# Attention's PSUM in two kinds of places, and b gates and sigmoids in the order of the rows, in a hybrid encoder layer

## The chip, the cores and the metric

The kernel runs on one core of a Trainium2 chip. The metric is the device time of one execution in microseconds (us): the median of three runs before is 1467.02 us (1465.7 to 1467.43). A profile is one further execution, taken by the hardware profiler. Five engines work side by side, each through its own list of instructions in a fixed order: PE (matmuls; its weight loads are listed as PEld), DVE and ACT (elementwise work, and the only readers of matmul results), POOL and SP (here mostly starting DMAs). An instruction that waits holds up everything behind it on its engine. Matmuls write to PSUM, eight banks of 128 partitions x 512 floats, of which all eight are given out in the part of the program that changes.

## The reference, cut to what matters

1024 new frames of one stream and 64 frames of a running one go through one layer. A combined projection feeds a gated convolution and a band attention; both results are weighted with sigmoid gates and merged:

```python
proj = xn @ w_in                       # cb, cc, ch, q, k, v, ga, gb
ya = (cb * causal_conv(cc * ch)) @ w_conv_out
o = band_attend(q, k, v, ...)          # 8 heads of 64, bias by relative distance, softmax
yb = o.reshape(B, L, ATT_DIM) @ w_attn_out
merged = sigmoid(ga) * ya + sigmoid(gb) * yb
x = x + merged @ w_out                 # then RMSNorm, SwiGLU FFN, residual, RMSNorm
```

A frame sees its own chunk of 64 frames and the eight before it, so a tile of 128 frames needs at most 640 keys, five blocks of 128.

## The kernel before

All products are in float32, each made of three matmuls on operands split into a high and a low part (`split`, lines 128 and 129: ACT casts the high part, DVE subtracts it to get the low part). The channels of the gates that the convolution half needs early are done before; what is left for the middle of the kernel is the b gate of all eight row blocks of 128 channels and the a gate of row blocks 6 and 7.

**The gates and attention run together.** `gate(i, cs)` computes row block i of `GATES` in pieces of 272 frames: 24 matmuls (`product`, lines 343 to 345) into one of three PSUM banks of pool `pmm`. A b gate is copied by ACT (line 908) and stored to `gb_d` by POOL (line 909); of the last two row blocks (a gates 6 and 7, tiles named g8 and g9) ACT takes the sigmoid straight out of the bank into `ga_rows` (line 905). Between the pieces the program advances `attention()` by 3.15 steps (`PER`). One step issues `scores` of a query tile, `transposed` of the tile two steps back, and every other time `values` of a pair of tiles. A scheduler then fixes the order of each engine, from these dependencies and its own estimates.

**A tile of attention.** `scores` puts up to 640 scores into a place of two banks; DVE adds the bias and takes the row's extreme in one custom instruction (line 964), ACT takes the exponential (line 974). `transposed` turns up to five blocks of 128x128 weights on PE (line 1053) into a place of two banks, and `split` takes them out in one cast and one subtraction (`pt`). Both kinds share one pool: `patt` has two places of two banks, handed out in turn to s and t. `values` (line 1078) has the eighth bank, in `ppv`. After a head's ninth tile, `rt` turns the nine columns of reciprocal row sums, ACT copies them to `rows`, and POOL stores them in four DMAs to `rc_d` (lines 1040 and 1044).

**The end of attention.** At i = 8 the pools of attention are closed. `ob`, the attention's output as a matmul operand, takes their place: its quarters 0 and 1 are cast from `o_rows` (tile names o0 and o1), which were scaled earlier; quarters 2 and 3 are loaded from `o_d` (line 1170), multiplied on DVE with `rc2` and `rc3`, the sums loaded back from `rc_d` (lines 1090 and 1172), and cast by ACT. `rows_in(m)` loads row block m of the b gate into a tile gb (line 1138) and of y into yg (line 1139), four of them here. The merge loop then goes over `MERGE = [6, 7, 0, 1, 2, 3, 4, 5]`: a sigmoid of gb on ACT (line 1194), the yb product on PE, multiply and add on DVE. `tc.issue_after(x)` puts what is issued under it behind instruction x in the schedule.

Of the kernel before, what the change touches and what calls it, by code (L numbers as in the profile page):

```python
# [8 lines left out]
F32 = mybir.dt.float32  # L9
F32R = mybir.dt.float32r  # L10
AF = mybir.ActivationFunctionType
# [4 lines left out]
P = 128  # L16
# [3 lines left out]
TS = 64  # L20
# [46 lines left out]
def encoder_kernel(ctx: ExitStack, tc: tile.TileContext, ins, outs):  # L67
    nc = tc.nc
    mm = nc.tensor.matmul
    vec, act, pool_e = nc.vector, nc.scalar, nc.gpsimd  # L70
# [13 lines left out]
    ident = const.tile([P, P], F32, name="ident")  # L84
# [41 lines left out]
    def split(hi, lo, src):  # L126

        a = act.copy(hi, src)  # L128
        b = vec.tensor_tensor(lo, src, hi.bitcast(F32), op=ALU.subtract)  # L129
        return a.ins, b.ins  # L130
# [214 lines left out]
            newest[0] = mm(out, b, p, start=False, stop=k == kt - 1).ins  # L345

    PIECES = [(j * HN, HN) for j in range(4)]
    GATES = [("b", m) for m in range(8)] + [("a", m) for m in range(6, 8)]
    for g, m in GATES:
        if m % 2 == 0:  # L350
            base = (C_GA if g == "a" else C_GB) + m * P
            ld = {"src": w_in[:, base : base + 2 * P], "w": 2 * P}
        plan.append((ld, KD, m % 2 * P))
    MERGE = [6, 7, 0, 1, 2, 3, 4, 5]
    for m in MERGE[::2]:
        ld = {"src": ins["w_attn_out"][0][:, m * P : (m + 2) * P], "w": 2 * P, "at": 40}
        plan += [(ld, 4, j * P) for j in range(2)]
# [483 lines left out]
    for n in range(len(units)):  # L841
# [26 lines left out]
        for _ in r:  # L868
            if n == 12:
                uforms(si)  # L870
            if n < 2 and si in (2 + n, 5 + n):
                i = 2 * n + si // 5
# [20 lines left out]
    patt = att_stack.enter_context(tc.tile_pool(name="patt", bufs=2, space=PSUM, reuse_waits="tile"))  # L893
# [4 lines left out]
    def gate(i, cs):  # L898
        g, m = GATES[i]
        for c in cs:  # L900
            o, n = PIECES[c]
            ps = pmm.tile([P, 512], F32, tag="mm", name=f"g{i}_{c}")
            product(ps[:, :n], gate_w[i], xn, o, n)
            if i >= len(GATES) - LAST:
                act.activation(ga_rows[m - 6][:, o : o + n], ps[:, :n], AF.Sigmoid)  # L905
                continue
            st = st_pool.tile([P, HN], F32, tag="st", name=f"gst{i}_{c}")
            act.copy(st[:, :n], ps[:, :n])
            nc.gpsimd.dma_start(gb_d[m * P : (m + 1) * P, o : o + n], st[:, :n])

    gate_w = {}

    heads, sums = {}, {}

# [75 lines left out]

    def scores(h, t):
        q, k, ks, v, vs, bias = heads[h]
        ps = patt.tile([P, 2, 512], F32, tag="att", name=f"s{h}_{t}")
        s = at_pool.tile([P, 640], F32, tag="s", name=f"p{h}_{t}", bufs=4)
        if t < 8:
            nb = min(t + 1, 5)
            k0, n, r = (t - nb + 1) * P, nb * P, P
            q0 = t * P if t < 4 else t * P + TS
        else:
            k, k0, n, r = ks, 0, CACHE + TS, TS  # L1000
            q0 = 512
        parts = 2 if n > 512 else 1
        w = n // parts
        for i in range(parts):
            ksl = slice(k0 + i * w, k0 + (i + 1) * w)
            mm(ps[:r, i, :w], q[0][:, q0 : q0 + r], k[:, ksl], start=True, stop=False)
            mm(ps[:r, i, :w], q[1][:, q0 : q0 + r], k[:, ksl], start=False, stop=True)  # L1007
        b0 = 640 - n if t < 8 else 0
        if t == 0:
            sums[h] = sm2[:, h % 2]  # L1010
        sm = sums[h]
        softmax(
            s[:r, :n], ps[:r, :, :w] if parts == 2 else ps[:r, 0, :w], bias[:r, b0 : b0 + n], sm[:r, t : t + 1],
            f"{h}_{t}",
        )
        return s
# [1 line left out]
    pts = {}  # L1018

    def transposed(h, t, s):  # L1020
        tp = patt.tile([P, 2, 512], F32, tag="att", name=f"t{h}_{t}").rearrange("p a b -> p (a b)")
        if t == 8:
            pt = at_pool.tile([P, 2, 5, TS], F32R, tag="pts", name=f"pts{h}", bufs=1)
            for i in range(4):
                nc.tensor.transpose(
                    tp[:, i * TS : (i + 1) * TS], s[:TS, i * P : (i + 1) * P], ident[:TS, :TS]
                )
            nc.tensor.transpose(tp[:TS, 512 : 512 + TS], s[:TS, 512:576], ident[:TS, :TS])
            split(pt[:, 0, :4, :], pt[:, 1, :4, :], tp[:, : 4 * TS].rearrange("p (b t) -> p b t", t=TS))
            split(pt[:TS, 0, 4, :], pt[:TS, 1, 4, :], tp[:TS, 512 : 512 + TS])  # L1030
            pts[h, 4] = pt

            sm = sums.pop(h)
            vec.reciprocal(sm, sm)
            tr = patt.tile([P, 2, 512], F32, tag="att", name=f"rt{h}")[:9, 0, :P]
            nc.tensor.transpose(tr, sm, ident)
            rows = at_pool.tile([P, P], F32, tag="rows", name=f"rows{h}", bufs=1)[:9]
            act.copy(rows, tr)
            for e in range(2):
                nc.gpsimd.dma_start(  # L1040
                    rc_d[h, e * HT : e * HT + 512].rearrange("(t p) -> t p", p=P), rows[4 * e : 4 * e + 4]
                )
                c = e * HT + 512
                nc.gpsimd.dma_start(rc_d[h : h + 1, c : c + 32], rows[8:9, 32 * e : 32 * e + 32])
            return
        g, j = divmod(t, 2)
        if j == 0:
            pts[h, g] = at_pool.tile([P, 2, 6, 256], F32R, tag="pt", name=f"pt{h}_{g}")
        pt = pts[h, g]
        nb = min(t + 1, 5)  # L1050
        b0 = t - nb + 1 - max(0, 2 * g - 4)
        for i in range(nb):
            nc.tensor.transpose(tp[:, i * P : (i + 1) * P], s[:, i * P : (i + 1) * P], ident)
        src = tp[:, : nb * P].rearrange("p (b t) -> p b t", t=P)
        js = slice(j * P, (j + 1) * P)
        split(pt[:, 0, b0 : b0 + nb, js], pt[:, 1, b0 : b0 + nb, js], src)

    def values(h, t):
        q, k, ks, v, vs, bias = heads[h]
# [76 lines left out]
    def rows_in(m):  # L1136
        t, z = rows[m] = u_rows.tile([P, T], F32, tag="yg", name=f"yg{m}"), row_tile((MERGE.index(m) % 5 + 1) % 2, f"gb{m}")
        nc.sync.dma_start(z, gb_d[m * P : (m + 1) * P])
# [8 lines left out]
    for i in range(4):  # L1147
# [3 lines left out]
        if i == 0:  # L1151
            prep(5)
    for i in range(4, len(GATES)):
        gate_w[i] = next_w()
        if i == len(GATES) - LAST:
            for _ in steps:
# [4 lines left out]
            t = uo.tile([P, 2, 4 * T + 8], F32R, name="ob")[:, :, : 4 * T]  # L1161
            ob = Acts(t.rearrange("p l (k t) -> p l k t", k=4))
            u_rows = pg_stack.enter_context(tc.tile_pool(name="u_rows", bufs=5, reuse_waits="tile"))
            ga_rows = [uo.tile([P, T], F32, name=f"ga{m}") for m in (6, 7)]
# [3 lines left out]
            for k, r in zip((2, 3), late_r):  # L1168
                o = ob.t[:, 0, k].bitcast(F32)
# [6 lines left out]
        for c in range(4):  # L1176
            gate(i, (c,))
            between()
        if i >= len(GATES) - LAST:
            m = GATES[i][1]  # L1180
            t = rows[m][0]
# [7 lines left out]
    for n, m in enumerate(MERGE):  # L1189
        wb = next_w()  # L1190
        if n + 4 < 8:
            rows_in(MERGE[n + 4])
        t, z = rows.pop(m)
        act.activation(z, z, AF.Sigmoid)
        late = t.rearrange("p (h n) -> p h n", h=2)[:, :, 512:]
        hi, lo = (ms[:, m, l].rearrange("p (h n) -> p h n", h=2) for l in range(2))
        for h in range(2):
            yb = psum2.tile([P, 2, 512], F32, tag="mm", name=f"yb{m}_{h}")
            for j in range(2):
                if n == 0:  # L1200
                    with tc.issue_after(gates_end):
                        product(yb[:, j, :HN], wb, ob, h * HT + j * HN, HN)
                else:
                    product(yb[:, j, :HN], wb, ob, h * HT + j * HN, HN)
            hs = slice(h * HT, (h + 1) * HT)
            zh, th = z[:, hs], t[:, hs]
            two = zh.rearrange("p (j n) -> p j n", j=2)
            vec.tensor_tensor(two, yb[:, :, :HN], two, op=ALU.mult)
            vec.tensor_tensor(th, th, zh, op=ALU.add)
            split(mg.at(0, m, h * HT, HT), mg.at(1, m, h * HT, HT), th)  # L1210
        pool_e.tensor_copy(hi, late)
        pool_e.tensor_tensor(lo, late, hi.bitcast(F32), op=ALU.subtract)
# [65 lines left out]
    if True:  # L1278
# [5 lines left out]
        for i in (0, 1, 2, 3, 8, 4, 5, 6, 7):  # L1284
            t0, n = TT[i]
            xt = wp.tile([P, D], F32, tag="xg", name=f"xr{i}")[:, :512]
            nc.sync.dma_start(xt[:n], x_rows(i)[:, :512])
            ps = bank2("BD", f"wo0_{i}")[:, 0]
# [373 lines left out]
    for n in range(1, len(names)):  # L1662
# [7 lines left out]
        if 2 <= n < 18:  # L1670
            nm, src = (("k", ck), ("v", cvv))[(n - 2) // 8]
            a = (n - 2) % 8 * 56
# [21 lines left out]
    bufs = {(hp, "hs"): 1, (hp, "snap"): 3, (hp, "sa"): 4, (hp0, "snap"): 1, (hp0, "sa"): 1}  # L1694
    for n, (i, d) in enumerate(order):
        if n < len(homes):
            pool, tag = homes[n]
# [33 lines left out]
    for b, ks in enumerate(blocks):  # L1731
        first, final = b == 0, b == len(blocks) - 1
        nk = blocks[b + 1] if not final else []
        for g in range(2):
            ps = {}
# [27 lines left out]
            for si, js in turns:  # L1763
                p, ht = STEPS[si], hts[base + si]
                key = {1: "A", 6: "A", 5: "A", 3: "A", 2: "B", 7: "D", 4: "D"}[p]
                for j in js:
                    i = 2 * g + j
                    if (key, j) not in ps:
                        ps[key, j] = psD.tile(
                            [P, 512], F32, tag="A" if key == "A" else "BD", name=f"{key}{b}_{i}",  # L1770
                            bufs=2 if key == "A" else 4,
                        )
                    t = ps[key, j]
                    ends = final and g == 1 and js == (1,) and si == len(STEPS) - 1
                    for c in ((slice(0, 256), slice(256, 512)) if ends else (slice(0, 512),)):
# [8 lines left out]
                    h, d, fresh = {  # L1784
                        1: (0, 0, 1), 2: (0, 0, 0), 6: (1, 0, 1), 7: (1, 1, 1), 5: (1, 1, 0), 4: (1, 0, 0), 3: (0, 1, 1),
                    }[p]
                    o = acc[i + 4 * h, d]
# [7 lines left out]
                    if final and si == 2:  # L1795
                        for hh, dd in ((0, 0), (1, 1), (1, 0), (0, 1)):
                            a = acc[i + 4 * hh, dd]
# [71 lines left out]
```

## Time and profile before

| | |
|---|---|
| median of three runs | 1467.02 us (1465.7 to 1467.43) |
| the profiled execution | 1467.9 us, of which the span from the first to the last instruction is 1466.1 |
| mean granted PE clock | 0.997 |
| gates alone | 384.9 to 411.5 us of the span |
| gates with attention | 411.5 to 591.3 |
| the last gates | 591.3 to 616.3 |
| the yb products of the merge | 616.3 to 664.3 |

How to read it: a busy share of PE near 100% does not say that PE could not be faster, since the ends of matmuls are modelled and overlap; the start-to-start times of matmuls say how fast it goes. A row of a group has line, engine, operation, output<-input, shape, count, then busy time and mean ns of one, then the idle time just before them and what ended it. A row of a timeline has start in us, duration in us, the instruction, how often it follows itself, and in brackets the idle time before it and its releaser. Rows of engine SPq or POOLq are the issue of a DMA, not its landing.

### The profile page before, as it was taken

How to read it: one execution, taken by the hardware profiler on the slowest of the kernel's cores; microseconds unless marked ns; L12 is line 12 of the kernel's file. 1: busy time of each engine (PE TensorE's matmuls, PEld its weight loads, DVE VectorE, ACT ScalarE, POOL GpSimd, SP SyncE). 2: the span in 40 equal slices, each digit the busy share in tenths (PEclk: the TensorE clock that was granted, in tenths of full speed). 3: DMA queues.
4: the chain of work that ended last, by engine and by line, in shares of the span. 5: the costliest groups of instructions: out<-in, count | busy, mean ns of one | idle time of the engine just before them, and what ended most of it. 6: DMA issues, size and time to landing. Idle time of an engine off the chain costs nothing.

```text
span 1466.1 us, 26257 instructions
## 1 busy us (share of the span) xinstructions
PE 1449.1 (99%) x10137; PEld 1362.2 (93%) x10137; DVE 993.3 (68%) x1831; ACT 679.7 (46%) x1354; POOL 154.4 (11%) x282
## 2 busy tenths in 40 slices
PE   8999999999999999999999999999999999999997
PEld 6899999999999989998889999999999998888886
DVE  7975565658357767473588667766666668957676
ACT  7644343336367667431355444444344445512223
POOL 1400010001221121111100111111011111000000
PEclk9999999999999999999999999999999999999999
DMA  8687612235877675743432444443334449877685
GB/s 286 182 276 226 197 56 71 67 111 200 261 214 195 177 189 150 260 149 126 156 108 80 160 162 157 151 168 129 122 130 169 148 179 313 274 232 249 210 266 204
DMA packets 156221, 262.47 MB, mean 179 GB/s; under 512 B 18529, under 2 KB 89377, under 8 KB 156097
## 3 DMA queue, kind: packets, MB, share of 16 engines
q1 hardware_dynamic: 132336, 184.33, 40.0%
q0 software_dynamic: 22608, 74.38, 14.2%
q10 hardware_dynamic: 1152, 2.10, 0.4%
q8 instruction: 79, 1.29, 0.4%
q14 instruction: 46, 0.37, 0.1%
HBM read 171.78 MB, written 90.81 MB: 179 GB/s over the span
## 4 chain that ended last, share of the span: by engine, by line
PE 92%; DVE 4%; DMA 2%; ACT 2%; issue 1%; ACTq 0%; SPq 0%; DVEq 0%
PE Ab L277 8%; PE Aa L277 8%; PE A L1779 7%; PE Da L277 4%; PE Db L277 4%; PE D L1779 3%; PE g L344 3%; PE g L345 3%; PE g L343 3%; PE Aga L277 2%; PE Ba L277 2%; PE Bb L277 2%; PE wo L1251 2%; PE wo L1253 2%; PE wo L1252 2%; PE B L1779 2%
## 5 line engine op out<-in xcount | busy, mean ns | idle before, releaser
L343 PE MATMUL g<-xn,wp 128*128 128x272 f32 x320 | 94.9, 297 | 2.3 <-ACT ga L905 2.3
L344 PE MATMUL g<-xn,wp 128*128 128x272 f32 x320 | 93.9, 293 | 0.0
L345 PE MATMUL g<-xn,low 128*128 128x272 f32 x320 | 93.7, 293 | 0.0
L128 ACT CAST ring<-w2r 128x512 fp32r<-128x512 f32 (+1 forms) x78 | 43.2, 588 | 98.8 <-PE A L1779 50.7
L964 DVE CUSTOM_DVE_ANT_0 p<-s,bb 128x640 f32<-128x640 f32 (+5 forms) x72 | 47.6, 662 | 38.9 <-PE s L1007 37.2
L1779 PE MATMUL A<-ring,ht 128*128 128x512 f32 (+1 forms) x267 | 72.5, 387 | 0.3 <-ACT acc L1792 0.3
L1779 PE MATMUL A<-ring,low 128*128 128x512 f32 (+1 forms) x270 | 72.6, 385 | 0.0
L129 DVE TENSOR_TENSOR low<-rawa,wa 128x512 fp32r<-128x512 f32 x55 | 37.7, 687 | 42.0 <-ACT wa L128 42.0
L343 PEld LDWEIGHTS g<-xn,wp 128*128 128x128 f32 x320 | 61.1, 191 | 3.1 <-ACT ga L905 2.5
L344 PEld LDWEIGHTS g<-xn,wp 128*128 128x128 f32 x320 | 61.1, 191 | 0.5
L345 PEld LDWEIGHTS g<-xn,low 128*128 128x128 f32 x320 | 61.0, 191 | 0.4
L1779 PEld LDWEIGHTS A<-ring,ht 128*128 128x128 f32 x267 | 49.7, 188 | 10.7 <-ACT acc L1792 0.7
L1779 PEld LDWEIGHTS A<-ring,low 128*128 128x128 f32 x270 | 50.2, 188 | 10.2
L129 DVE TENSOR_TENSOR ring<-w2r,ring 128x512 fp32r<-128x512 f32 (+1 forms) x78 | 49.1, 647 | 14.1 <-ACT ring L128 14.1
L277 PE MATMUL Ab<-tt,wb 128*128 128x272 f32 x352 | 57.8, 286 | 0.4 <-ACT wb L128 0.4
L277 PE MATMUL Ab<-mg,wb 128*128 128x272 f32 x352 | 58.0, 286 | 0.0
L277 PE MATMUL Aa<-mg,wa 128*128 128x272 f32 x352 | 57.7, 285 | 0.0
L277 PE MATMUL Aa<-tt,wa 128*128 128x272 f32 x352 | 57.7, 285 | 0.0
L974 ACT ACTIVATE p<-p,mx 128x640 f32<-128x640 f32 (+5 forms) x72 | 50.8, 706 | 13.7 <-DVE mx L964 13.2
L128 ACT CAST wa<-rawa 128x512 fp32r<-128x512 f32 x55 | 34.0, 621 | 47.4 <-PE Ab L277 33.3
L129 DVE TENSOR_TENSOR pt<-t,pt 128x640 fp32r<-128x640 f32 (+2 forms) x64 | 41.8, 653 | 15.6 <-ACT pt L128 14.7
L128 ACT CAST wb<-rawb 128x512 fp32r<-128x512 f32 x55 | 34.0, 620 | 38.4 <-PE Aa L277 24.2
(591 smaller groups left out, 4507.8 us busy)
## 6 DMA issues: line engine op xcount, KB each, us to landing
h_d<-hq POOLq DMA_DIRECT2D x44, 512.0 KB, 3.9
ht<-h_d SPq DMA_DIRECT2D x77, 256.0 KB, 3.6
low<-h_d SPq DMA_DIRECT2D x77, 256.0 KB, 4.2
h_d<-hq_early POOLq DMA_DIRECT2D x29, 512.0 KB, 4.2
rawa<-in_w_ff SPq DMA_DIRECT2D x11, 1024.0 KB, 5.6
rawb<-in_w_ff SPq DMA_DIRECT2D x11, 1024.0 KB, 5.3
w2r<-in_w_ff SPq DMA_DIRECT2D x11, 1024.0 KB, 8.1
qd<-q_d SPq DMA_DIRECT2D x32, 272.0 KB, 4.2
```

The source lines that it names most:

```text
L128: a = act.copy(hi, src)
L129: b = vec.tensor_tensor(lo, src, hi.bitcast(F32), op=ALU.subtract)
L277: newest[0] = mm(t[:, j, :HN], w[:, k, :], x[p][:, k, l, j * HN : (j + 1) * HN], start=p in (1, 2, 7) and k == 0 and n == 0, stop=k == las ...
L343: mm(out, a, first, start=k == 0, stop=False)
L344: mm(out, a, then, start=False, stop=False)
L345: newest[0] = mm(out, b, p, start=False, stop=k == kt - 1).ins
L964: vec.tensor_tensor_reduce(out=s if len(ps.shape) == 2 else s.rearrange("p (a b) -> p a b", a=2), in0=ps, in1=bias if len(ps.shape) == 2 e ...
L974: act.activation(s, s, AF.Exp, bias=mx, scale=-1.0, accum_out=sm)
L1251: mm(ps, x(k, 0), wh, start=f, stop=False)
L1252: mm(ps, x(k, 1), wh, start=False, stop=False)
L1253: mm(ps, x(k, 0), wl, start=False, stop=e)
L1779: mm(t[:, c], ht[k][:, j, x], w[:, l, c], start=p in (1, 2, 7) and k == 0 and n == 0, stop=k == len(ks) - 1 and n == 2, skip_group_check=p ...
```

## The change

Three edits. (1) `scores` gets a place of its own, one of two banks, under the tag s; `transposed` gets two places of one bank each, under the tag t, so that a tile of four or five blocks is turned into two places, three blocks and then one or two, each with its own cast and subtraction. The number of banks stays eight. (2) The b gates are computed in the order of `MERGE`, 6 and 7 first. (3) The sigmoids of the b gates in the merge loop are put behind the last sigmoid of an a gate.

```diff
-    GATES = [("b", m) for m in range(8)] + [("a", m) for m in range(6, 8)]
+    MERGE = [6, 7, 0, 1, 2, 3, 4, 5]
+    GATES = [("b", m) for m in MERGE] + [("a", m) for m in range(6, 8)]
...
             if i >= len(GATES) - LAST:
-                act.activation(ga_rows[m - 6][:, o : o + n], ps[:, :n], AF.Sigmoid)
+                gate_out[0] = act.activation(ga_rows[m - 6][:, o : o + n], ps[:, :n], AF.Sigmoid).ins
...
-        ps = patt.tile([P, 2, 512], F32, tag="att", name=f"s{h}_{t}")
+        ps = patt.tile([P, 2, 512], F32, tag="s", name=f"s{h}_{t}", bufs=1)
...
-        tp = patt.tile([P, 2, 512], F32, tag="att", name=f"t{h}_{t}").rearrange("p a b -> p (a b)")
+        def bank(nm):
+            return patt.tile([P, 512], F32, tag="t", name=nm)
...
-            tr = patt.tile([P, 2, 512], F32, tag="att", name=f"rt{h}")[:9, 0, :P]
+            tr = bank(f"rt{h}")[:9, :P]
...
-        for i in range(nb):
-            nc.tensor.transpose(tp[:, i * P : (i + 1) * P], s[:, i * P : (i + 1) * P], ident)
-        src = tp[:, : nb * P].rearrange("p (b t) -> p b t", t=P)
         js = slice(j * P, (j + 1) * P)
-        split(pt[:, 0, b0 : b0 + nb, js], pt[:, 1, b0 : b0 + nb, js], src)
+        for a, b in ((0, nb),) if nb < 4 else ((0, 3), (3, nb)):
+            tp = bank(f"t{h}_{t}_{a}")
+            for i in range(a, b):
+                nc.tensor.transpose(tp[:, (i - a) * P : (i - a + 1) * P], s[:, i * P : (i + 1) * P], ident)
+            src = tp[:, : (b - a) * P].rearrange("p (b t) -> p b t", t=P)
+            split(pt[:, 0, b0 + a : b0 + b, js], pt[:, 1, b0 + a : b0 + b, js], src)
...
-        act.activation(z, z, AF.Sigmoid)
+        with tc.issue_after(gate_out[0]):
+            act.activation(z, z, AF.Sigmoid)
```

On ACT, where attention ends and the last gates run, the order before is this (gb7 is the b gate's row block 7, g8 and g9 the PSUM tiles of the a gates 6 and 7, piece by piece; wp are weights of the yb products):

```order
L1194 ACT_TABLE_LOAD
L1194 ACTIVATE gb7_7113<-gb7_7113 128x1088
L128 CAST ob_7084<-o0_6819 128x1088
L128 CAST ob_7084<-o1_6862 128x1088
L905 ACTIVATE ga6_7088<-g8_0_7124 128x272
L905 ACTIVATE ga6_7088<-g8_1_7150 128x272
L905 ACTIVATE ga6_7088<-g8_2_7176 128x272
L128 CAST wp14_0_7555<-rawp14_7415 128x512
L128 CAST ob_7084<-rc2_7094 128x1088
L905 ACTIVATE ga6_7088<-g8_3_7202 128x272
L128 CAST wp15_0_7623<-rawp14_7415 128x512
L128 CAST ob_7084<-rc3_7095 128x1088
```

In the changed program the same place on ACT reads:

```order
L128 CAST ob_7204<-o0_6924 128x1088
L128 CAST ob_7204<-o1_6967 128x1088
L905 ACT_TABLE_LOAD
L905 ACTIVATE ga6_7208<-g8_0_7244 128x272
L905 ACTIVATE ga6_7208<-g8_1_7270 128x272
L905 ACTIVATE ga6_7208<-g8_2_7296 128x272
L128 CAST ob_7204<-rc2_7214 128x1088
L128 CAST wp14_0_7675<-rawp14_7535 128x512
L128 CAST ob_7204<-rc3_7215 128x1088
L905 ACTIVATE ga6_7208<-g8_3_7322 128x272
L128 CAST wp15_0_7743<-rawp14_7535 128x512
L905 ACTIVATE ga7_7209<-g9_0_7354 128x272
```

The sigmoid of gb7 has gone from the front, and the sigmoid of g8_3 now stands behind the cast of quarter 3 of ob (ob<-rc3), where it stood ahead of it.

On PE, in head 1, between the transposes of query tiles 4 and 5 (g3_2 is a piece of a gate), the order before is:

```order
L1053 MATMUL t1_4_5020<-ident_75,p1_4_4943 128x128 x5
L1078 MATMUL pv1_3_5029<-pt1_1_4952,vd1_4594 128x512 x3
L1078 MATMUL pv1_3_5029<-pt1_1_4952,vd1_4594 128x2x128
L1006 MATMUL s1_7_5040<-kd1_4584,qd1_0_4578 128x320
L1007 MATMUL s1_7_5040<-kd1_4584,qd1_1_4581 128x320
L1006 MATMUL s1_7_5040<-kd1_4584,qd1_0_4578 128x320
L1007 MATMUL s1_7_5040<-kd1_4584,qd1_1_4581 128x320
L343 MATMUL g3_2_5088<-xn01_99,wp3_0_4378 128x272
L344 MATMUL g3_2_5088<-xn01_99,wp3_0_4378 128x272
L345 MATMUL g3_2_5088<-xn01_99,low_95 128x272
L343 MATMUL g3_2_5088<-xn01_99,wp3_0_4378 128x272
L1053 MATMUL t1_5_5049<-ident_75,p1_5_4968 128x128 x5
```

And in the changed program:

```order
L1059 MATMUL t1_4_0_5039<-ident_75,p1_4_4958 128x128 x3
L1059 MATMUL t1_4_3_5045<-ident_75,p1_4_4958 128x128 x2
L1083 MATMUL pv1_3_5050<-pt1_1_4966,vd1_4594 128x512 x3
L1083 MATMUL pv1_3_5050<-pt1_1_4966,vd1_4594 128x2x128
L343 MATMUL g3_2_5115<-xn01_99,wp3_0_4378 128x272
L1006 MATMUL s1_7_5061<-kd1_4584,qd1_0_4578 128x320
L1007 MATMUL s1_7_5061<-kd1_4584,qd1_1_4581 128x320
L1006 MATMUL s1_7_5061<-kd1_4584,qd1_0_4578 128x320
L1007 MATMUL s1_7_5061<-kd1_4584,qd1_1_4581 128x320
L1059 MATMUL t1_5_0_5070<-ident_75,p1_5_4983 128x128 x3
L1059 MATMUL t1_5_3_5076<-ident_75,p1_5_4983 128x128 x2
```

The five transposes are two groups, and one gate matmul stands between tile 4's and tile 5's where four stood.

On SP, which starts the loads and some of the stores, the order at the end of attention before is (co are pieces of the attention's output on their way to `o_d`):

```order
L985 DMA o_d_92<-co7_2_6983 64x256
L1138 DMA gb7_7113<-gb_d_91 128x1088
L985 DMA o_d_92<-co7_3_7052 64x256
L1090 DMA rc3_7095<-rc_d_93 64x1088
L989 DMA o_d_92<-co7_s_7064 64x32 x2
L1170 DMA ob_7084<-o_d_92 128x1088 x2
```

And in the changed program:

```order
L1143 DMA gb7_7233<-gb_d_91 128x1088
L985 DMA o_d_92<-co7_2_7100 64x256
L985 DMA o_d_92<-co7_3_7172 64x256
L1095 DMA rc3_7215<-rc_d_93 64x1088
L989 DMA o_d_92<-co7_s_7184 64x32 x2
L1175 DMA ob_7204<-o_d_92 128x1088 x2
```

Only the load of gb7 has moved ahead; it reads what a gate near the start of attention stored, where before it read what the last b gate stored.

On DVE and ACT the changed program has 40 more instructions each, the second parts of five tiles in each of eight heads. From the transpose of head 7's sums on, PE's order is the same in both; ACT's, DVE's, POOL's and SP's are the same from the merge loop's first tiles on.

More of the change, by code (lines that the diff above doesn't have):

```diff
@@ L353, in encoder_kernel @@
         plan.append((ld, KD, m % 2 * P))
-    MERGE = [6, 7, 0, 1, 2, 3, 4, 5]
     for m in MERGE[::2]:
@@ L909, in gate @@
             nc.gpsimd.dma_start(gb_d[m * P : (m + 1) * P, o : o + n], st[:, :n])
-    gate_w = {}
+    gate_w, gate_out = {}, [None]
     heads, sums = {}, {}
@@ L1020, in transposed @@
     def transposed(h, t, s):
-        tp = patt.tile([P, 2, 512], F32, tag="att", name=f"t{h}_{t}").rearrange("p a b -> p (a b)")
+        def bank(nm):
+            return patt.tile([P, 512], F32, tag="t", name=nm)
         if t == 8:
+            tp = bank(f"t{h}_{t}")
             pt = at_pool.tile([P, 2, 5, TS], F32R, tag="pts", name=f"pts{h}", bufs=1)
@@ L1027, in transposed @@
                 )
-            nc.tensor.transpose(tp[:TS, 512 : 512 + TS], s[:TS, 512:576], ident[:TS, :TS])
+            nc.tensor.transpose(tp[:TS, 4 * TS : 5 * TS], s[:TS, 512:576], ident[:TS, :TS])
             split(pt[:, 0, :4, :], pt[:, 1, :4, :], tp[:, : 4 * TS].rearrange("p (b t) -> p b t", t=TS))
-            split(pt[:TS, 0, 4, :], pt[:TS, 1, 4, :], tp[:TS, 512 : 512 + TS])
+            split(pt[:TS, 0, 4, :], pt[:TS, 1, 4, :], tp[:TS, 4 * TS : 5 * TS])
             pts[h, 4] = pt
```

## Prediction

> **What bounds the kernel now.** I read the page first, then the busy time of each engine by stretches, then the stretch in which PE stands still.
>
> ```profile
> span 1466.1 us, 26257 instructions
> PE 1449.1 (99%) x10137; PEld 1362.2 (93%) x10137; DVE 993.3 (68%) x1831; ACT 679.7 (46%) x1354; POOL 154.4 (11%) x282
> ```
>
> PE is busy for all but 17 us. The change takes no matmul away, so it can only win back time in which PE waits, or runs at a lower clock. The next view cuts the span into stretches; the columns are length, busy us (and count) of PE, PEld, DVE, ACT and POOL, PE's granted clock, DMA share and GB/s.
>
> ```profile
> 411.50:591.30 179.80, 178.60 (x1278) 164.61 (x1278) 129.62 (x327) 125.64 (x313) 32.74 (x60) 1.00 0.68 182
> ...
> 597.24:599.67 2.43, 0.16 (x2) 0.00 (x0) 1.44 (x2) 2.41 (x4) 0.00 (x0) 1.00 0.73 143
> 599.67:603.56 3.89, 3.89 (x18) 3.89 (x19) 2.25 (x2) 1.15 (x3) 0.00 (x0) 0.56 0.80 241
> ...
> 616.30:664.30 48.00, 48.00 (x386) 48.00 (x385) 35.79 (x53) 18.85 (x28) 6.91 (x16) 1.00 0.52 178
> ```
>
> The last row, the yb products, gives the pace that PE can hold: 384 matmuls of 272 columns (the row's 386 hold two of a neighbour) in 48.0 us, 0.125 us each, so a gate piece of 24 takes 3.0 us. The two middle rows are the place that the change aims at: 2.43 us in which PE does nothing, then 3.89 us in which it does 18 matmuls at a granted clock of 0.56. PE's timeline there, the tiles of the a gates:
>
> ```profile
> 597.11 0.29 PE L345 MATMUL g<-xn,low 128*128 128x272 f32 x1
> 599.67 0.39 PE L343 MATMUL g<-xn,wp 128*128 128x272 f32 x1 [2.27 <-ACT ga L905]
> ...
> 600.18 0.43 PE L343 MATMUL g<-xn,wp 128*128 128x272 f32 x1
> 600.41 0.43 PE L344 MATMUL g<-xn,wp 128*128 128x272 f32 x1
> ...
> 603.36 0.36 PE L345 MATMUL g<-xn,low 128*128 128x272 f32 x1
> 603.56 0.29 PE L343 MATMUL g<-xn,wp 128*128 128x272 f32 x1
> ```
>
> The fourth piece (g8_3) needs the bank of the first (g8_0), which ACT had not yet read. Half a microsecond after the restart the starts are 0.23 us apart instead of 0.125, until 603.36. ACT's timeline says why it came late:
>
> ```profile
> 591.24 0.21 ACT L980 COPY ca_s<-pv 64x64 f32<-64x64 f32 x1 [1.92 <-PE pv L1065]
> 594.80 1.28 ACT L1194 ACT_TABLE_LOAD   x1 [3.35 <-DMA gb<-gb_d]
> 596.10 1.11 ACT L1194 ACTIVATE gb<-gb 128x1088 f32<-128x1088 f32 x1
> 597.12 2.08 ACT L128 CAST ob<-o 128x1088 fp32r<-128x1088 f32 x2
> 599.22 0.98 ACT L905 ACTIVATE ga<-g 128x272 f32<-128x272 f32 x3
> ...
> 604.70 0.39 ACT L905 ACTIVATE ga<-g 128x272 f32<-128x272 f32 x1
> ...
> 608.44 1.11 ACT L128 CAST ob<-rc 128x1088 fp32r<-128x1088 f32 x1 [2.84 <-DVE rc L1172]
> ```
>
> ACT sat 3.35 us in front of a b gate's sigmoid, for its load, with the casts of ob and the a gates' sigmoids queued behind.
>
> **Term 1, the gap goes.** In the changed order the two casts of ob follow the copy of ca_s, then the table load, then the sigmoid of g8_0. From the end of that copy at 591.45: 2.08 + 1.28 + 0.39 gives 595.2, and PE asks for the bank at 597.24, two microseconds later. So the 2.43 us go, and with them the slow stretch: 18 matmuls take 18 x 0.125 = 2.25 us instead of 3.89, 1.64 less. Together **4.07 us**. Unseen is whether the casts could have started at 591.45, since the sigmoid hid it; their sources were scaled long before, and the place of ob was last read by the work that ends with that copy. The other end, casts that start at 597.12 as now, is a rival below.
>
> [...]
>
> **Term 2, a new wait, later.** In the changed order the sigmoid of g8_3 stands behind the cast of ob's last quarter (ob<-rc3), where before it ran at 604.70, ahead of it. g9_2 needs the bank of g8_3. Without the gap PE asks for it after three more pieces, at 597.24 + 9.0 = 606.24. When is the cast done? Its chain runs through two transfers:
>
> ```profile
> 596.23 0.46 SPq L1090 DMA_DIRECT2D rc<-rc_d  x1
> ...
> 598.13 2.51 SPq L1170 DMA_DIRECT2D ob<-o_d  x2
> ```
>
> ```profile
> SPq L1090 <- DMA rc_d<-rows: 5.4, 1, 5.4
> ```
>
> ```profile
> L1044 POOL DMA_DIRECT2D rc_d<-rows x16: 505/506/524, 435.4 to 589.8; - x16
> ...
> DMA to landing us min/median/max: 3.1/4.3/7.3
> ```
>
> ```profile
> 602.37 1.29 DVE L1172 TENSOR_TENSOR rc<-ob,rc 128x1088 f32<-128x1088 f32 x1 [1.64 <-DMA ob<-o_d]
> ...
> 607.11 1.29 DVE L1172 TENSOR_TENSOR rc<-ob,rc 128x1088 f32<-128x1088 f32 x1 [2.85 <-DMA ob<-o_d]
> ```
>
> The stores of the sums are started up to 589.8; SP waits 5.4 us for them and starts the load of rc3 at 596.23. SP's queue holds the stores of co_s and both loads of ob behind it, so all of them move with it. The second quarter is in at 607.11; then 1.29 us on DVE, 1.11 for the cast (from 608.44), 0.39 for the sigmoid and 0.05 to PE: 610.0. As late as that, PE would wait 3.7 us. But this execution had both transfers slow: the store took 6.4 us where the median of its kind is 4.3, and while it was under way the load of gb7 ran, which the change moves ahead. Of the loads of ob this answer gives:
>
> ```profile
> DMA to landing us min/median/max: 4.2/5.5/6.8
> ```
>
> With the median store the chain ends 2.1 us sooner, at 607.9, and PE waits 1.6; with the middle of the two loads 1.3 sooner again, a wait of 0.3. I take the middle of these, **0.9 us**; ends 0 and 3.7. Whether such a wait costs clock too is open: 2.43 us did; I take none, and 1.64 as the other end.
>
> **Term 3, attention.** What PE visibly waited for in its 179.8 us (engine, line <- whom: us, times, longest):
>
> ```profile
> PEld t L1053 <- DVE pt L129: 2.3, 7, 0.4
> ...
> PEld s L1006 <- DVE mx L964: 1.2, 4, 0.5
> ...
> PE t L1053 <- DVE pt L129: 0.7, 4, 0.2
> ...
> PE s L1006 <- DVE mx L964: 0.3, 1, 0.3
> ```
>
> That is 4.5 us, all that this part can give. 3.0 are transposes that wait for the subtraction of the tile before, and the smaller places ease them; 1.5 are scores that wait for DVE, which the change doesn't help, since s went into one place nearly always before too. Against it, the scheduler has used the ease up: in the order shown one gate matmul covers the way from tile 4's transposes to tile 5's, where four did. I take **1.5 us**, half of the transposes' share; ends 0 and 4.5. The price of the cut, by shape:
>
> ```profile
> L129 DVE TENSOR_TENSOR pt<-t,pt 128x640 fp32r<-128x640 f32 x32 | 26.3, 823 | 11.1 <-ACT pt L128 10.6
> ...
> L129 DVE TENSOR_TENSOR pt<-t,pt 128x384 fp32r<-128x384 f32 x8 | 4.5, 556 | 1.7 <-ACT pt L128 1.4
> ...
> L129 DVE TENSOR_TENSOR pt<-t,pt 128x256 fp32r<-128x256 f32 x8 | 3.3, 416 | 0.4 <-ACT pt L128 0.4
> ```
>
> ```profile
> L128 ACT CAST pt<-t 128x640 fp32r<-128x640 f32 x32 | 22.1, 690 | 12.4 <-PE t L1053 12.2
> ...
> L128 ACT CAST pt<-t 128x384 fp32r<-128x384 f32 x8 | 3.8, 477 | 3.3 <-PE t L1053 3.2
> ...
> L128 ACT CAST pt<-t 128x256 fp32r<-128x256 f32 x8 | 3.0, 373 | 1.8 <-PE t L1053 1.7
> ```
>
> 556 + 416 - 823 = 149 ns more on DVE for a cut tile and 477 + 373 - 690 = 160 on ACT; over 40 tiles 6.0 and 6.4 us (four-block tiles taken alike). Both engines have room in this stretch, 179.8 - 129.6 = 50 us on DVE and 54 on ACT, so I cost it at nothing.
>
> **The rest at nothing.** The order of the b gates changes addresses, not sizes. The eight sigmoids now run after the last a gate: four of 1.11 us delay the first cast of the merged operand, wanted about 3.0 (a yb tile of 24 matmuls) + 1.4 us after the gates' end, to about 0.4 + 4.4. PE's second yb place covers 3.0 us, and DVE is busy 35.8 of the 48.0 us there; without that cover it would cost some 0.4.
>
> **Sum.** -4.07 + 0.9 - 1.5 = -4.7. Against the profiled execution's own 1467.9 that is 1463.2; it lies 0.9 above the median shown, so I forecast 1467.0 - 4.7 = **1462.3**.
>
> **Rivals.** *The wait only moves* (0.20). Either the chain of rc3 is as late as in this trace, and PE waits 3.7 us at g9_2 and loses 1.64 of clock again: -4.07 + 5.3 - 1.5 = -0.2, 1466.8. Or the casts of ob can't start before 597.12, and with the table load behind them the gap grows by 1.3 instead of going; g9_2 then finds its bank free, and -1.5 + 1.3 gives the same. For the first speaks that the order puts the sigmoid there, against it the medians. *All goes well* (0.08): no second wait, all 4.5 us of attention: -8.6, 1458.5. *The slow stretch stays* (0.04), if the gap isn't its cause: -2.43 + 0.9 - 1.5 = -3.0, 1464.0. *Slower* (0.06): the cut tiles lie on PE's path. If the next transposes and scores come late by the whole extra 0.309 us of each of 40 tiles, that is +12.4, and -4.07 + 0.9 + 12.4 = +9.2, 1476.2; it decides from 0.08 us a tile (3.2 / 40). For it: the waits above are for DVE. Against it: a part's subtraction can start while ACT casts the next, and DVE idled 11.1 us ahead of the whole tiles' subtractions. [...]
>
> **Chances.** The forecast has 0.62. The measurement can tell about 0.2%, 2.9 us, from no change. Faster by more: nine tenths of the forecast, the good case and half of the stretch that stays, 0.66; within: the rest of these and the moved wait, 0.27; slower 0.07. The range runs from the good case to just over the moved wait, 1458.5 to 1467.2, and leaves out the slower case and a few hundredths beyond its ends.
>
> **What would show it.** Term 1: the sigmoid of g8_0 near 595, PE without a break at 597.24 and no row with a lowered clock there. Term 2: idle time ahead of the seventh of the eight a-gate pieces, released by ACT; its size is the arrival of ob's last quarter less 606.24, all taken from attention's end. Term 3: attention's stretch shorter than 179.8 us, fewer us of t behind pt, mean times of 556 and 416 ns for the parts. I am wrong if ACT waits between 591 and 595, if the second wait is longer than 2.4 us, or if scores wait for DVE by more than 1.5 us.

## The result, and the profile after

The changed kernel takes **1463.58 us** (median of 14 runs, 1462.44 to 1467.28) beside 1467.36 for the kernel before (14 runs, 1465.27 to 1470.57): ratio 0.9978, 95% interval 0.997 to 0.9985. The profiled execution took 1463.62 us against 1467.9. Its page begins:

```profile
span 1461.7 us, 26326 instructions
...
PE 1447.1 (99%) x10137; PEld 1359.9 (93%) x10137; DVE 997.7 (68%) x1871; ACT 682.6 (47%) x1394; POOL 154.5 (11%) x282
```

The same matmuls, 2.0 us less of busy PE and 4.4 us less span; DVE and ACT have the 40 instructions more. The stretches of the prediction, with the same bounds in us (length, then busy us and count of PE, PEld, DVE, ACT, POOL, then clock, DMA share, GB/s):

```profile
411.50:591.30 179.80, 178.34 (x1281) 164.37 (x1281) 133.01 (x369) 129.21 (x354) 32.74 (x60) 1.00 0.70 191
597.24:599.67 2.43, 2.43 (x22) 2.43 (x21) 0.09 (x1) 0.00 (x0) 0.00 (x0) 1.00 0.67 238
599.67:603.56 3.89, 3.89 (x33) 3.89 (x32) 2.46 (x3) 1.62 (x2) 0.81 (x1) 1.00 0.97 346
```

Where PE stood still it now does 22 matmuls, and where it crept it does 33 instead of 18, at a granted clock of 1.00 instead of 0.56. The stretch of attention has hardly moved. ACT's timeline at the end of attention:

```profile
590.36 0.21 ACT L980 COPY ca_s<-pv 64x64 f32<-64x64 f32 x1 [1.93 <-PE pv L1070]
590.67 2.10 ACT L128 CAST ob<-o 128x1088 fp32r<-128x1088 f32 x2
592.79 1.28 ACT L905 ACT_TABLE_LOAD   x1
594.09 0.69 ACT L905 ACTIVATE ga<-g 128x272 f32<-128x272 f32 x2
...
604.23 1.10 ACT L128 CAST ob<-rc 128x1088 fp32r<-128x1088 f32 x1 [1.70 <-DVE rc L1177]
605.23 0.39 ACT L905 ACTIVATE ga<-g 128x272 f32<-128x272 f32 x1
```

ACT goes from the copy into the casts of ob, the table load and the first a gates without a wait: g8_0 is read at 594.09. Eleven microseconds later the sigmoid of g8_3 stands behind the cast of ob's last quarter, and PE's timeline has its only break there, ahead of g9_2:

```profile
605.20 0.29 PE L345 MATMUL g<-xn,low 128*128 128x272 f32 x1
605.68 0.39 PE L343 MATMUL g<-xn,wp 128*128 128x272 f32 x1 [0.19 <-ACT ga L905]
605.91 0.29 PE L344 MATMUL g<-xn,wp 128*128 128x272 f32 x1
```

From start to start that is 0.48 us instead of the 0.12 of its neighbours, 0.36 lost; the matmul behind it comes another 0.1 late. Last, the waits of PE and its weight loads in the stretch of attention (us, times, longest), all that the view lists:

```profile
PEld s L1006 <- DVE mx L964: 3.8, 13, 0.5
...
PE s L1006 <- DVE mx L964: 1.1, 4, 0.3
...
PEld t L1028 <- DVE pt L129: 0.4, 1, 0.4
...
PEld t L1059 <- DVE pt L129: 0.3, 1, 0.3
...
PEld t L1059 <- ACT p L974: 0.2, 1, 0.2
```

The transposes, which waited 3.0 us for pt at line 1053, wait 0.3 at the same place of the code, now line 1059 (and 0.4 at line 1028, where before had this row):

```profile
PEld t L1025 <- DVE pt L129: 0.3, 2, 0.2
```

The scores, which waited 1.5, wait 4.9. All rows of PE and PEld in this view add up to 5.9 us before and to 5.8 in the changed kernel: the waits have changed places.

PE's timeline of every execution can be cut at three starts: the first score, the last value product, the first yb product. This gives "attention" and "last gates" below, and is how two kernels are compared from here on. Before the first score the two profiled executions differ by 0.52 us (411.96 and 411.44); two executions of one kernel (E4 and E9 below) differ there by 1.21, so that is not the change's.

| kernel | edits | median us | ratio to before, 95% interval | attention | last gates |
|---|---|---|---|---|---|
| before | none | 1467.36 | | 178.92 | 25.41 |
| after | 1, 2, 3 | 1463.58 | 0.9978, 0.997 to 0.9985 | 178.55 | 21.79 |
| E1 | 1 | 1467.36 | 1.001, 1.0001 to 1.0018 | 178.85 | 25.52 |
| E2 | 2, 3 | 1464.07 | 0.9983, 0.9974 to 0.9993 | 178.98 | 21.33 |
| E3 | 3 | 1464.81 | 0.999, 0.9982 to 0.9999 | 178.76 | 21.38 |
| E4 | 2 | 1463.93 | 0.9981, 0.9972 to 0.9989 | 178.73 | 21.33 |
| E5 | 1, 2, 3, cast later | 1464.3 | 0.9989, 0.998 to 0.9998 | 178.77 | 21.32 |
| E6 | 1 uncut, 2, 3 | 1465.62 | 0.9994, 0.9985 to 1.0003 | 181.27 | 20.68 |
| E7 | 1 in three, 2, 3 | 1464.7 | 0.9989, 0.9981 to 0.9998 | 180.13 | 21.08 |
| E8 | 1, 2, 3 again | 1463.41 | 0.9976, 0.9968 to 0.9985 | 179.28 | 21.43 |
| E9 | 2 again | 1463.74 | 0.9982, 0.9973 to 0.9991 | 178.71 | 21.31 |

E1 to E4 were timed on one chip, E5 to E7 on one, E8 and E9 on one, each set beside the kernel before (1467.27, 1466.49 and 1466.64 us there). The recorded ratios differ a little from the quotients of the medians (for E1, 1467.36 / 1467.27 is 1.0001).

### The profile page after: what moved, and what is told of

It is laid out like the page before. It is cut to its first block, busy times and chain, and to the rows that moved or that the text cites. A ratio compares the mean times of both kernels' runs of the same rounds, so it can differ in the third digit from the quotient of the medians.

```text
span 1461.7 us, 26326 instructions
## 1 busy us (share of the span) xinstructions
PE 1447.1 (99%) x10137; PEld 1359.9 (93%) x10137; DVE 997.7 (68%) x1871; ACT 682.6 (47%) x1394; POOL 154.5 (11%) x282
## 4 chain that ended last, share of the span: by engine, by line
PE 90%; DVE 4%; DMA 3%; ACT 1%; issue 1%; POOL 0%; SPq 0%; ACTq 0%; DVEq 0%; POOLq 0%
PE Ab L277 9%; PE Aa L277 8%; PE A L1785 7%; PE Da L277 4%; PE Db L277 4%; PE D L1785 3%; PE Aga L277 2%; PE g L345 2%; PE g L343 2%; PE g L344 2%; PE Bb L277 2%; PE Ba L277 2%; PE wo L1257 2%; PE wo L1259 2%; PE wo L1258 2%; PE B L1785 2%
## 5 line engine op out<-in xcount | busy, mean ns | idle before, releaser
L1257 PE MATMUL wo<-low,mg 128*128 128x512 f32 x128 | 50.9, 397 | 0.0
```

The lines of the kernel that those rows point to most:

```text
L1257: mm(ps, x(k, 0), wh, start=f, stop=False)
```

## The experiments

### E1 to E4: the edits apart

E1, the places of the banks alone (the diff's edit 1 on the kernel before):

```diff
-        ps = patt.tile([P, 2, 512], F32, tag="att", name=f"s{h}_{t}")
+        ps = patt.tile([P, 2, 512], F32, tag="s", name=f"s{h}_{t}", bufs=1)
...
+            return patt.tile([P, 512], F32, tag="t", name=nm)
...
+        for a, b in ((0, nb),) if nb < 4 else ((0, 3), (3, nb)):
```

> Edit 1 alone (places of attention), b gates and sigmoids as before. My theory: the gap of 2.4 us ahead of g8_3 and the stretch at a lowered clock stay, since ACT's order at the end of attention is that of before; attention itself gains little: its stretch from the first score to the last pv, 178.9 us before and 178.5 in the changed kernel, stays within 0.5 us of 178.5. Time 0 to 1 us under before, ratio 0.9995. Rival (attention's places are worth the 1.5 us that I forecast, and the profile of the changed kernel missed it): 1.5 us or more under before, ratio 0.999 or lower.

1467.36 us, ratio 1.001. PE's timeline, where the gap was:

```profile
596.61 0.29 PE L345 MATMUL g<-xn,low 128*128 128x272 f32 x1
599.39 0.59 PE L343 MATMUL g<-xn,wp 128*128 128x272 f32 x1 [2.50 <-ACT ga L905]
599.79 0.43 PE L344 MATMUL g<-xn,wp 128*128 128x272 f32 x1
600.01 0.43 PE L345 MATMUL g<-xn,low 128*128 128x272 f32 x1
```

and ACT's, with the reason:

```profile
594.53 1.28 ACT L1199 ACT_TABLE_LOAD   x1 [3.58 <-DMA gb<-gb_d]
595.82 1.11 ACT L1199 ACTIVATE gb<-gb 128x1088 f32<-128x1088 f32 x1
```

The gap is there with its cause, 2.78 us from start to start, and again matmuls start 0.22 to 0.23 us apart behind it, from 599.79 to 602.51, and 0.12 to 0.13 from 602.67 on. Attention is 0.07 us shorter than before. Edit 1 alone gains nothing; the interval puts it 0.1 to 1.8 thousandths on the slow side, with the medians 0.09 us apart.

E2, the order of the b gates and the place of their sigmoids, with attention's banks as before:

```diff
-    GATES = [("b", m) for m in range(8)] + [("a", m) for m in range(6, 8)]
+    MERGE = [6, 7, 0, 1, 2, 3, 4, 5]
+    GATES = [("b", m) for m in MERGE] + [("a", m) for m in range(6, 8)]
...
+                gate_out[0] = act.activation(ga_rows[m - 6][:, o : o + n], ps[:, :n], AF.Sigmoid).ins
...
-        act.activation(z, z, AF.Sigmoid)
+        with tc.issue_after(gate_out[0]):
+            act.activation(z, z, AF.Sigmoid)
```

> Edits 2 and 3 without edit 1 (b gates in the rows' order, sigmoids behind the last a gate's; attention as before). My theory: all of the gain that a measurement shows is here: from the last pv to the first yb product 21.5 to 22.5 us where before had 25.4, no lowered clock, a short wait at g9_2 behind ACT. Time 3 to 4 us under before, ratio 0.9975. Rival (both halves are needed for it): 1 to 2 us.

1464.07 us; last gates 21.33, no gap, and no wait at g9_2 either. All of the gain that can be told is here. E3 and E4 have one of the two edits each:

```diff
...
+                gate_out[0] = act.activation(ga_rows[m - 6][:, o : o + n], ps[:, :n], AF.Sigmoid).ins
...
-        act.activation(z, z, AF.Sigmoid)
+        with tc.issue_after(gate_out[0]):
+            act.activation(z, z, AF.Sigmoid)
```

> Edit 3 alone: sigmoids behind, b gates in their old order. ACT's order is that of the changed kernel, but the load of gb7 stands late on SP again, beside the stores of the sums. My theory on the forecast's second wait: with that load in the way, the stores take 6 us again, the cast of ob's last quarter ends near 18.5 us after the last pv, and PE waits at g9_2 for 2.5 to 3.7 us, with a lowered clock behind it: from the last pv to the first yb product 24 to 27 us, ratio 0.9985 to 1.0005. Rival (the load of gb7 does not matter, the stores are fast or slow by chance): as the changed kernel, 21.8 us and ratio 0.9975.

```diff
-    GATES = [("b", m) for m in range(8)] + [("a", m) for m in range(6, 8)]
+    MERGE = [6, 7, 0, 1, 2, 3, 4, 5]
+    GATES = [("b", m) for m in MERGE] + [("a", m) for m in range(6, 8)]
```

> Edit 2 alone: b gates in the rows' order, sigmoids where they were. The sigmoid of gb7 stands at the front of ACT again, but its load was started early. My theory (the wait for the load was the cause, not the sigmoid's place): ACT goes on at once, table load 1.28 + sigmoid 1.11 + two casts 2.08 + 0.39 end some 4.9 us after the copy of ca_s, 1 us before PE asks; no gap, no lowered clock, and no wait at g9_2 since g8_3's sigmoid stands ahead of the last cast of ob: from the last pv to the first yb product 21.3 us, ratio 0.9970 to 0.9978. Rival (the sigmoid's place is what counts): a gap remains, 1 us or more ahead of g8_3, ratio 0.999.

Either one alone removes the gap. ACT's timeline in E4, where the sigmoid of gb stands at the front as before:

```profile
588.76 1.28 ACT L1194 ACT_TABLE_LOAD   x1
590.06 1.11 ACT L1194 ACTIVATE gb<-gb 128x1088 f32<-128x1088 f32 x1
591.07 0.19 ACT L980 COPY ca_s<-pv 64x64 f32<-64x64 f32 x1
591.17 2.10 ACT L128 CAST ob<-o 128x1088 fp32r<-128x1088 f32 x2
593.30 0.40 ACT L905 ACTIVATE ga<-g 128x272 f32<-128x272 f32 x1
```

It is no obstacle there: its load was started early, it runs even ahead of attention's last copy, and g8_0 is read at 593.30. So the sigmoid's place did no harm once its data had come, and E3 shows the other half: the late load did none once the work that frees PE's banks no longer stood behind the wait for it. In E3, where the load stayed late, I had expected a wait of 2.5 to 3.7 us at g9_2 and a lowered clock. The profile shows neither (PE's starts from 596 to 607 are 0.12 to 0.13 us apart, but for one of 0.20 at g9_2):

```profile
604.45 1.10 ACT L128 CAST ob<-rc 128x1088 fp32r<-128x1088 f32 x1 [1.10 <-DVE rc L1172]
605.46 0.39 ACT L905 ACTIVATE ga<-g 128x272 f32<-128x272 f32 x1
```

The sigmoid of g8_3 was just in time: it ends at 605.85, and PE asks 15.3 us after the last value product (605.32 less 590.00 in the changed kernel, with 0.12 behind the matmul at 605.20), which was at 590.62 here, so at 605.9. E3's median is 0.7 to 0.9 above E2's and E4's; the intervals overlap, and one profile cannot say whether other executions of it do wait.

### E5: the cast behind the sigmoid

```diff
-                split(ob.t[:, 0, k], ob.t[:, 1, k], r)
+                if k == 2:
+                    split(ob.t[:, 0, k], ob.t[:, 1, k], r)
...
+        if i == len(GATES) - LAST:
+            with tc.issue_after(gate_out[0]):
+                split(ob.t[:, 0, 3], ob.t[:, 1, 3], late_r[1])
```

> The changed kernel, with the cast of ob's last quarter and its subtraction put behind the sigmoid of g8_3 on ACT and DVE. If the 0.36 us that PE waited at g9_2 came from that cast standing ahead of the sigmoid, the wait goes: the last gates (last value product to first yb product) take 21.3 to 21.4 us where the changed kernel took 21.79, no idle time over 0.2 us there, and the time falls by 0.3 to 0.5 us, to about 1463.3. Rival: the wait has another cause (the sigmoids of the a gates queue behind the table load); then it stays at 0.3 to 0.5 us and the time too.

The second wait went (last gates 21.32, no break), and the kernel was no faster: 1464.3 us, and in the profile PE takes 843.25 us from the first yb product to the last matmul, where it took 841.63. What SP, ACT and PE say of it, each in its own view:

```profile
SPq L1143 <- DVE ob L129: 7.9, 1, 7.9
```

```profile
619.58 1.11 ACT L1204 ACTIVATE gb<-gb 128x1088 f32<-128x1088 f32 x1 [2.04 <-DMA gb<-gb_d]
620.60 0.63 ACT L128 CAST mg<-yg 128x544 fp32r<-128x544 f32 x1
```

```profile
PEld yb L343 <- DVE gb L1218: 0.8, 2, 0.5
PE yb L343 <- DVE gb L1218: 0.3, 1, 0.3
```

The subtraction that moved with the cast was what SP waited for with one of the next loads of gb (6.5 us in the changed kernel). The load came later, and its sigmoid sat 2.04 us at the head of ACT with a cast of mg behind it. DVE's multiply, which frees the place of a yb tile, came late with that, and PE waited for it. It is the shape of the first gap over again, some 20 us on; it cost 1.1 us within the first 300 matmuls of yb, against the 0.4 won. By the last matmul it is 1.6, but that stretch differs by 0.7 between two executions of the changed kernel (841.63 and, in E8, 840.96), and the profiled execution of E5 was the slowest of its eleven (1465.61), so the size is that of this execution.

### E6 and E7: the cut

E6 keeps the places of their own but turns a tile uncut, into one place of two banks; E7 cuts five blocks into two, two and one, and four into two and two:

```diff
E6
-            return patt.tile([P, 512], F32, tag="t", name=nm)
+            return patt.tile([P, 1024], F32, tag="t", name=nm, bufs=1)
-        for a, b in ((0, nb),) if nb < 4 else ((0, 3), (3, nb)):
+        for a, b in ((0, nb),):
E7
-        for a, b in ((0, nb),) if nb < 4 else ((0, 3), (3, nb)):
+        for a, b in ((0, nb),) if nb < 4 else ((0, 2), (2, 4), (4, nb))[: nb - 2]:
```

> The changed kernel with the turned weights uncut, in one place of two banks; the scores keep their own place of two banks. Theory: the extra pieces on DVE and ACT are what made the scores wait (4.9 us in the changed kernel, 1.5 before); without them the scores' waits fall to about 1.5 us, the transposes' waits come back to about 3, and attention takes 178.7 to 179.0 us, as before the change. Rival: the scores wait because they have only one place; then their waits stay at 4 to 5 us, the transposes' 3 come on top, and attention takes 181 to 182 us.

> The changed kernel with the five-block tiles' turned weights in three pieces (two, two and one block) and the four-block tiles' in two and two. Theory that the pieces delay the scores: one more piece of a five-block tile adds some 150 ns on DVE and 160 on ACT for each of 32 tiles, the scores' waits rise from 4.9 us to 7 or more, and attention grows from 178.55 us by 1 to 4. Rival, that the pieces cost nothing and the scores' waits come from their single place: the waits stay near 4.9 us and attention within 0.4 us of 178.55.

Their waits in attention, E6 first:

```profile
PEld t L1059 <- DVE pt L129: 2.9, 8, 0.7
...
PEld s L1006 <- DVE mx L964: 1.3, 5, 0.5
PE t L1059 <- DVE pt L129: 1.3, 5, 0.5
PEld t L1059 <- ACT rows L1041: 0.7, 4, 0.2
...
PE s L1006 <- DVE mx L964: 0.3, 1, 0.3
```

```profile
PEld t L1059 <- DVE pt L129: 2.8, 10, 0.3
PEld s L1006 <- DVE mx L964: 1.9, 9, 0.4
PEld t L1028 <- DVE mx L964: 1.1, 3, 0.4
...
PE s L1006 <- DVE mx L964: 0.2, 1, 0.2
```

In E6 the scores wait 1.6 us: a single place alone does not make them wait 4.9. But the transposes wait 4.2 for pt, more than the 3.0 with shared places, and attention grows to 181.27. Five gate matmuls (0.6 us) have moved into attention there, so the two stretches are better taken together: 201.95 us in E6, 200.34 in the changed kernel, 200.31 in E2 with the shared places. **By these profiles places of their own cost some 1.6 us, and the cut gives about as much back**, which would be why edit 1 comes out at nothing. E6 is one profile; the four of shared places with the gap gone (E2, E3, E4, E9) have 200.02 to 200.31 and the two of the changed kernel 200.34 and 200.71, so the cost is 1.6 to 1.9 and the cut's return 1.2 to 1.6. Neither theory had that; the rival had attention's time (181 to 182) but not the wait that it was to come from. E7 fells the theory that the pieces delay the scores, and its rival too: with 32 more pieces the scores wait 2.1 us, neither 7 nor 4.9, and the transposes wait again. Attention did grow by the 1 to 4 us of the theory, but by other waits. Attention and last gates together take 201.21, 0.5 to 0.9 more than in the two profiles of the changed kernel (200.34 and, in E8, 200.71).

### E8 and E9: the changed kernel and the order alone, again

Neither has an edit beside those named: E8 is the changed kernel, E9 is E4.

> The changed kernel once more, beside the kernel with the b gates' order alone. If the 0.36 us wait at g9_2 is set by how fast the sums' stores land in one execution (3.9 us in the profile of the changed kernel, 2.3 where the wait was absent), this look shows no wait when the last store lands within 3 us and a wait of 0.3 to 1 us when it takes 4 or more. Rival: the wait belongs to the changed kernel in every execution, whatever the stores take. Attention again 178.5 to 178.8 us; time as the kernel with the order alone within 0.1%.

> The b gates' order alone, once more, on the same chip as the changed kernel. If the places of the banks and the sigmoids' place give nothing beside the order, both times lie within 0.1% (1.5 us) of each other and both 3 to 4 us under the kernel before. Rival: the places give the 0.4 us that one profile of attention showed, and the sigmoids' place 0.3 or more; then the changed kernel is 0.5 to 1 us faster than this one.

1463.41 and 1463.74 us, 0.33 apart with overlapping intervals: edits 1 and 3 add nothing to edit 2 that can be told. E8's wait at g9_2 is 0.1 us (last gates 21.43 against 21.33). SP's wait for the stores of the sums, changed kernel, E8 and E4, in that order:

```profile
SPq L1095 <- DMA rc_d<-rows: 2.8, 1, 2.8
```

```profile
SPq L1095 <- DMA rc_d<-rows: 2.9, 1, 2.9
```

```profile
SPq L1090 <- DMA rc_d<-rows: 0.8, 1, 0.8
```

So the wait is not the same in every execution, but the rule I had written does not tell why: from issue to landing the stores took 3.6 and 3.3 us in E8 (medians of two of each size) and 3.9 and 3.6 in the changed kernel's first profile, between the rule's bounds of 3 and 4 in both, and SP waited as long. The few tenths arose behind them: from the last value product to the cast of rc3 it is 13.88 us in E8 (591.19 to 605.07) and 14.23 in the first profile (590.00 to 604.23), with the load of rc3 started even 0.17 later after that product.

E8's attention is also the longest of all but E6 and E7, and in its list of waits stands one of the scores for DVE that is 1.0 us long, twice the longest of the first profile. DVE's timeline there:

```profile
567.83 0.41 DVE L982 TENSOR_TENSOR co<-pv,ca 64x256 f32<-64x256 f32 x1
569.70 1.29 DVE L1109 TENSOR_TENSOR o<-o,rc 128x1088 f32<-128x1088 f32 x1 [1.46 <-issue]
...
571.29 0.67 DVE L964 CUSTOM_DVE_ANT_0 p<-s,bb 128x512 f32<-128x512 f32 x1
```

The early scaling of o, whose operands come by DMA, stands ahead of the scores' custom instruction and was 1.46 us late (0.61 in the first profile); the view does not show what released it.

With the shared places (E2, E4, E9) SP waits 0.8 to 0.9 us for these stores, in the changed kernel, E5 and E8 2.7 to 2.9. The places of their own are not enough for that: in E6, which has them, the stores land in 1.5 us and SP does not wait for them. Why was not tried.

## Why the prediction was right, and where not

The forecast was a gain of 4.7 us, to 1462.3; measured are 3.8 (1467.36 to 1463.58), and 3.2 in the last set (1466.64 to 1463.41). Time and sign were within what was stated, and the sum was too large by about one microsecond. In the two profiles term 1 came as forecast, term 3 gave 1.1 us less (0.37 instead of 1.5), and term 2 cost about 0.4 less (0.45, the 21.79 of the last gates less 25.41 - 4.07, instead of 0.9). That the error of term 2 made up for part of that of term 3 is luck.

**Term 1, the gap goes (4.07): right, with its cause.** The 2.43 us and the half clock are both gone; 25.41 - 4.07 + the 0.36 lost at g9_2 gives 21.70 for the last gates, and 21.79 were measured; the 0.1 behind the break makes up the rest. The unseen assumption, that the casts of ob could start with the end of the copy of ca_s, holds: copy until 590.57, casts from 590.67. That the half clock (0.50 granted from 600.10 to 603.50 in the kernel before) came from the gap is shown from both sides: E1, with the gap, has starts 0.22 to 0.23 us apart behind it; E3 and E4, without, have 0.12 to 0.13 but for one of 0.20 in E3, the profiles of E2 to E4 have a mean granted clock of 0.999 where those of before and E1 have 0.997, and the last gates of E2 to E4 are 4.1 to 4.2 us shorter than E1's, where the idle time alone was 2.5. What I did not see is that edit 2 or edit 3 alone would do: the wait needed both a late load and work queued behind it.

**Term 2, a new wait later (0.9): the mechanism right, the size too large.** The wait is ahead of the seventh of eight a-gate pieces and released by ACT's sigmoid, behind the cast of rc3, as put; it is 0.36 us in one profile and 0.1 in another, without any lowered clock (1.00 granted from 605.68 to 610 in the first; starts 0.12 to 0.13 us apart behind it in E8). The argument for taking the stores as faster than in the trace of before (SP waited 5.4 us there, 2.8 now) carried the choice. The reason given with it, that the load of gb7 ran beside them, is borne out in part: with the load moved and the old places SP's wait is 0.8 to 0.9, with the load late 4.0 in E3; but in the changed kernel about 2 us of that come back, for a reason that stays open, and E1 breaks the pattern (0.5, after SP had been held 3.9 us by something else).

**Term 3, attention (1.5): the step that failed.** The profile of the changed kernel has 0.37 us, E1 against before 0.07, E8 is 0.36 slower than before: nothing. The table holds more than these: in attention PE's order is the same in the four profiles with edit 1 as it stands (changed kernel, E1, E5, E8) and the same in the five without it, and the means are 178.86 and 178.82 us. The failed step is "1.5 are scores that wait for DVE, which the change doesn't help, since s went into one place nearly always before too". It took the places of their own as free and let the transposes' ease stand alone. The transposes' waits did fall, by more than the half I took (3.0 to 0.3 at the place named), but the scores' rose by 3.4. That is no chance of one profile: they wait 4.9 to 6.7 us in the four with edit 1 and 1.5 to 1.8 in the five without. Nor were the 4.5 us "all that this part can give", since the whole list had 5.9. E6 shows what the places of their own cost without the cut (about 1.6 us), and the changed kernel that the cut pays about that. Where the scores' wait comes from is narrowed, not settled: a single place is not enough for it (E6), and it does not grow with the number of pieces (E7), but both of these have an order of PE of their own. What remains as a candidate is the order. In PE's timeline 36 groups of transposes came straight behind a gate matmul before, 16 do now, and 47 instead of 33 come straight behind scores: the room that the cut made may have been used up in the list of instructions. The prediction named this as the point against the term and gave it half. It is not shown, since no run changed the places and held the order fixed.

**The rest at nothing: right.** From the first yb product to the last matmul 841.54 us before, 841.63 after; the four sigmoids run as one block of 4.10 us at 612.67 on ACT, and PE has no break behind them. The cut cost what the rows of before said, and nothing on the path:

```profile
L129 DVE TENSOR_TENSOR pt<-t,pt 128x384 fp32r<-128x384 f32 x48 | 26.5, 551 | 4.9 <-ACT pt L128 3.4
L128 ACT CAST pt<-t 128x384 fp32r<-128x384 f32 x48 | 23.0, 480 | 10.9 <-PE t L1059 10.0
L129 DVE TENSOR_TENSOR pt<-t,pt 128x256 fp32r<-128x256 f32 x40 | 16.6, 415 | 0.4
L128 ACT CAST pt<-t 128x256 fp32r<-128x256 f32 x40 | 14.9, 373 | 0.9 <-PE t L1059 0.9
```

551 and 415 ns on DVE (556 and 416 before). The slower rival, that the pieces lie on PE's path with 0.309 us each, would have made E7 slower by 32 x 0.309 = 9.9 us; it is slower by 0.5 to 0.9. Of "wrong if", one sign did come: the scores waited for DVE by more than 1.5 us.

None of the kernels tried beats the changed one; all of its gain that can be told is had with edit 2 alone (E4, E9).

## What to carry to other kernels

An instruction that waited for a DMA at the head of an engine's list held up what was queued behind it (3.35 us on ACT in the kernel before, 2.27 us of idle PE with it): look at what stands behind the wait before looking at the wait, since either an earlier load (E4) or another place in the list (E3) cured it, with last gates of 21.33 and 21.38 us instead of 25.41, and moving work behind it can build the same wait further on (2.04 us on ACT in E5). The waits that a change removes from a list are its gain only while no other wait takes the room: here the transposes' fell by 2.7 us and the scores' rose by 3.4. Splitting a buffer into places of their own can cost time by itself, as E6 suggests (1.6 to 1.9 us by its one profile), and should be priced before the gain is counted.

## What the hardware showed

An idle PE of 2.27 us in the kernel before (the bracket of its row; 2.43 us were lost) and of 2.50 in E1 was followed by a stretch of slower matmuls. Before, the granted clock was 0.50 from 600.10 to 603.50, 3.4 us, with starts 0.23 us apart; in E1 the starts were 0.22 to 0.23 us apart from 599.79 to 602.51, 2.7 us. The break at g9_2 (0.19 us idle, 0.36 lost) was followed by none: the granted clock was 1.00 from 605.68 to 610. Two executions of one kernel differed by 0.73 us in attention alone (178.55 and 179.28), so a single profile cannot carry a term of half a microsecond.
